# Soft mixture of eight experts: all seven outer products of a Strassen-Winograd scheme split on a second level, as 110 equal tasks

## The chip, the cores and the metric

The kernel runs on one core of a Trainium2 chip. The metric is the device time of one execution in microseconds (us); the median of several executions is compared. Engines are named as in the profile: PE (TensorE matmuls), PEld (its weight loads), DVE (VectorE), ACT (ScalarE), POOL (GpSimd) and SP (SyncE). POOL and SP also issue the DMAs; a DMA that casts or that adds to its destination is issued on POOL.

## The reference

```python
x: [16, 512, 512] f32, router_logits: [16, 512, 8] f32, expert_weights: [8, 512, 2048] f32
probs = softmax(router_logits)                     # over the 8 experts
for e in range(8):
    output += probs[:, :, e:e+1] * np.matmul(x, expert_weights[e])    # [16, 512, 2048] f32
```

Seen as one product: out [8192 rows, 2048] = A [8192, 4096] times B [4096, 2048], where A holds the eight copies of x, each row scaled by that row's probability of the expert, and B holds the experts' weights one above the other. Matmuls run in f16 with sums in f32.

## The kernel before

**The outer scheme.** Rows are taken in half blocks of 256 (`HQ`), an even and an odd one to each of 16 row blocks `q` (or `i`); the experts are cut into two halves (p1 for the first four experts, p2 for the last four, pq for their sum), the columns into two halves of 1024. That is a 2x2 by 2x2 block product, computed with seven block products P1 to P7 instead of eight (Strassen-Winograd). The left factors are products of x and probabilities (`z` tiles in f16, made on DVE from `xT` and `pT`) and differences of these; the right factors are the weights B11, B12, B21, B22 and the sums T1 = B12-B11, T2 = B22-T1, T3 = B22-B12, T4 = T2-B21 (signs as the code has them). P1 uses B11, P2 B21, P5 T1, P6 T2, P3 B22, P4 T4, P7 T3.

**The inner level.** A block product of 256 rows by 1024 columns over two pairs of experts can be split again in the same way, into seven products of 128 rows by 512 columns over 8 steps of 128, 56 matmuls of 128x512 instead of the plain 64. This needs sums of the left factors (`s1`, `s2`, `s4`) and of the weights (`inner_sums`, `inner_weights`: four sums of 128x4096).

**What is split before.** Of the seven products, P1 (from q=2 on), P5, P2 and P4 run one after another through `sub_product`, each with the inner level, over pairs of half blocks; results go to DRAM (`kept` 1, 5 and 2, and P4's into `out`). The first 128 matmuls (q=0,1 of P1) are plain. While a product runs, the generator `prep` of the next one (`weights_of_t1`, `weights_of_21`, `weights_of_t4`, `weights_of_main`) loads expert weights through POOL (with a cast to f16), makes the T sums in tiles of 128x4096 and stores those that are wanted later. `pinned` is False here: the scheduler orders DVE and ACT.

Then `for q in range(NI)` (16 row blocks, `pinned` True, order written by hand) runs P6 and P7 plain, 64 matmuls each, and P3 with the inner level (plain in q=0): 184 matmuls a row block. Kept results are read back by SP (`load_kept`), added in PSUM seeds (ACT) or on DVE (`tt`), and `put` (line 594) sends the outputs, on POOL's queue; the block (1,0) is added to P4's result by an accumulating DMA, 64 in all.

**Names and lines in the profile.** Line 122 is `tt`, every two-operand operation of DVE; 142 is `mm`, the matmuls; 133 `sp` and 136 `pool` are DMAs of the two queues; 404, 627, 649, 669, 718 and 729 are copies by ACT. `w` are weight tiles (15 buffers of 128x4096 f16), `z` left factors (10 buffers of 128x2048 f16), `h` f32 results and seeds, `ps` banks of PSUM, `xT` and `pT` the transposed x and the probabilities.

Of the kernel before, what the change touches and what calls it, by code (L numbers as in the profile page):

```python
# [11 lines left out]
def kernel(  # L33
# [6 lines left out]
):  # L40
    nc = tc.nc
    P = 128
# [10 lines left out]
    NB = 512  # L53
# [12 lines left out]
    zpool = ctx.enter_context(tc.tile_pool(name="zpool", bufs=10))  # L66
# [11 lines left out]
    def share(**sizes):  # L78

        order = sorted(used, key=used.get)  # L80
        for use, n in sizes.items():
            places[use], order = [order[:n], 0], order[n:]
# [26 lines left out]
    pinned = [True]  # L109

# [3 lines left out]
    def dve(i):  # L114
        note(i)
        if pinned[0]:
            tc.keep_in_program_order(i)

    act = dve
# [15 lines left out]
    def pool(o, i):  # L135
        note(nc.gpsimd.dma_start(out=o, in_=i))  # L136
# [9 lines left out]
    stored = {}  # L146
# [3 lines left out]

    def cast_w(q, kn, e, t, parts=1):
        k, n = kn
        for c in range(0, C, C // parts):
            pool(t[:, ds(e * C + c, C // parts), :],
                 expert_weights[(q // 10 - 1) * HE + 2 * k + e, ds(c * P, C * P // parts),
                                ds((q % 10 - 1) * NH + n * NB, NB)].rearrange("(c p) n -> p c n", p=P))

    def load(what, kn, gate=True):
        t = new_w()
        if gate:  # L160
            dve(nc.vector.memset(t.rearrange("p (e c) n -> p e c n", e=2)[:, :, 0, 0:2], 0.0))  # L161
        if (what, kn) in stored:
            pool(t, stored[what, kn])
        else:
            for e in range(2):
                cast_w(what, kn, e, t)
        return t

    def store(what, kn, t):
        stored[what, kn] = d = dram.tile([P, K8, NB], f16, name=f"wd{what}_{kn[0]}{kn[1]}")  # L170
        sp(d, t)

    def inner_sums(b, t3=None):

        t3 = t3 or b[0, 1]
        w = {1: b[0, 0], 2: b[1, 0], 3: b[1, 1], 7: t3}

        def step(p, x, y):
            if p not in w:
                w[p] = new_w()  # L180
            tt(w[p], x, y, SUB)
        return w, [lambda: step(5, b[0, 1], b[0, 0]), lambda: step(6, b[1, 1], w[5]),
                   lambda: step(4, w[6], b[1, 0]), lambda: step(7, b[1, 1], b[0, 1])]

    def inner_weights(b):
        w, sums = inner_sums(b)
        sums[0]()
        yield
        sums[1]()
        sums[2]()  # L190
        yield
        sums[3]()
        return w

# [16 lines left out]
    P2, P1, PQ = 0, HE, 2 * HE  # L211

# [37 lines left out]
    def diag(p):  # L250

        d = h_tile([P, 4, P], f16)
        tt(d, ident.unsqueeze(1).to_broadcast([P, 4, P]), p.to_broadcast([P, 4, P]), MUL)
        return d
# [39 lines left out]

    R = 4
# [21 lines left out]

    x_dram = {}
# [14 lines left out]
    def store_x():  # L333
        while x_new:
            h, xT = x_new.pop()
            x_dram[h] = dram.tile([P, C, HQ], f16, name=f"x_{h}")
            sp(x_dram[h], xT)

# [5 lines left out]
    def mul(xT, pT, e0, ne, t0, nt):  # L344
        z = zpool.tile([P, ne, C, nt], f16, name="z", tag="z")
        tt(z, xT[:, :, ds(t0, nt)].unsqueeze(1).to_broadcast([P, ne, C, nt]),
           pT[:, ds(e0, ne), ds(t0, nt)].unsqueeze(2).to_broadcast([P, ne, C, nt]), MUL)
        return z.rearrange("p e c t -> p (e c) t")


    kept = {r: [dram.tile([2, HQ, NB], f32, name=f"kept{r}_{i}") for i in range(NI)] for r in (1, 2, 5)}

    def half(use="any"):
        return h_tile([P, NB], f32, use)

    def out_rows(i, odd, u, cols, n):
        return out_f[ds((2 * i + odd) * HQ + u * P, P), ds(cols * NH + n * NB, NB)]

    def to_kept(r, i, u, n, t):
        if r == 4:  # L360
            sp(out_rows(i, 1, u, 0, n), t)
        else:
            sp(kept[r][i][n, ds(u * P, P), :], t)

    def from_kept(r, i, u, n, use):
        t = half(use)
        sp(t, kept[r][i][n, ds(u * P, P), :])
        return t

    def sub_product(r, odd, first, w, prep, start=0, xp=None, rest=()):  # L370

        for d in range(start, NI // 2):
            hs = [4 * d + odd, 4 * d + 2 + odd]
            xp = xp or [(load_x(h), load_p(h, first)) for h in hs]
            a11, a12 = (mul(*xp[0], e0, 2, 0, HQ) for e0 in (0, 2))
            a21, a22 = (mul(*xp[1], e0, 2, 0, HQ) for e0 in (0, 2))
            xp = None

            def new(a, b, op):
                z = zpool.tile([P, K8, HQ], f16, name="z", tag="z")  # L380
                tt(z, a, b, op)
                return z
            s1 = new(a21, a22, ADD)
            s2 = new(s1, a11, SUB)
            s4 = new(a12, s2, SUB)
            tt(a21, a11, a21, SUB)
            for make in rest:
                make()
            rest = ()
            z = {1: a11, 2: a12, 3: s4, 4: a22, 5: s1, 6: s2, 7: a21}  # L390

            for u in range(HQ // P):
                banks = {}

                def prod(p, b, start=True):
                    if start:
                        banks[b] = bank()
                    for k in range(K8):
                        mm(banks[b], z[p][:, k, ds(u * P, P)], w[p][:, k, :], start and k == 0, k == K8 - 1)
                    return banks[b]  # L400

                def keep(ps):
                    t = half("r")
                    nc.scalar.copy(t, ps)  # L404
                    return t

                def put(t, n, a, b, op):
                    o = half("o")
                    tt(o, a, b, op)
                    to_kept(r, 2 * d + t, u, n, o)  # L410

                r1 = keep(prod(1, "x"))
                put(0, 0, prod(2, "b"), r1, ADD)
                r5 = keep(prod(5, "q"))
                r2 = keep(prod(6, "x", False))
                put(0, 1, prod(3, "q", False), r2, ADD)
                prod(7, "x", False)
                r3 = keep(banks["x"])
                put(1, 1, banks["x"], r5, ADD)
                put(1, 0, r3, prod(4, "d"), SUB)  # L420
            with behind():
                store_x()
                next(prep, None)
        for _ in prep:
            pass

    ready = {}


    def finish(g):  # L430
        try:
            while True:
                next(g)
        except StopIteration as e:
            return e.value
# [5 lines left out]
    early_z0(1, ds_[1])  # L441
    for n in range(2):
        ps = [bank() for _ in range(4)]
        for e in range(HE):
# [8 lines left out]
            if n == 1:  # L453
                for j in ((4, 5), (6, 7), (), ())[e]:
                    early_xp1(j, ds_[j - 4])
                if e == 1:
                    sums[0]()
        for j in range(4):
            o = half()
            act(nc.scalar.copy(o, ps[j]))  # L460
            sp(kept[1][j // 2][n].rearrange("(p j) m -> j p m", j=2)[j % 2], o)
        if n == 0:
# [3 lines left out]
            w, sums = inner_sums(b11, new_w())  # L466

    def weights_of_t1():
        b = {}
        for i, kn in enumerate(BLOCKS):  # L470
            b[kn] = load(12, kn)
            yield
            tt(b[kn], b[kn], b11[kn], SUB)
            store("t1", kn, b[kn])
        yield
        ready[5] = yield from inner_weights(b)
    pinned[0] = False
    x_new.extend((4 + 2 * t, xp1[t][0]) for t in range(2))
    share(xs=3, r=4, o=8)
    sub_product(1, 0, P1, w, weights_of_t1(), 1,  # L480
                xp1, (sums[1], sums[3], sums[2]))


    def weights_of_21():
        b = {}
        yield
        for kn in BLOCKS:
            b[kn] = load(21, kn)
            yield
            store(21, kn, b[kn])  # L490
        yield
        ready[2] = yield from inner_weights(b)
    sub_product(5, 1, PQ, ready[5], weights_of_21())


    def weights_of_t4():
        b = {}
        for i, kn in enumerate(BLOCKS):
            t, t2 = load(22, kn), load("t1", kn)
            if i < 3:  # L500
                b[kn] = load(21, kn)
            yield
            tt(t2, t, t2, SUB)
            store(22, kn, t)
            store("t2", kn, t2)
            if i == 3:
                b[kn] = load(21, kn)
                yield
            tt(b[kn], b[kn], t2, SUB)
# [263 lines left out]
```

## Time and profile before

| | |
|---|---|
| times of three executions | 1432.79, 1433.21, 1433.62 us, median 1433.21 |
| span of the profiled execution | 1431.8 us |
| median time less that span | 1.4 us |
| granted clock of TensorE | 1.000 |
| matmuls 128x512 / 128x256 (z and w) | 6544 / 16 |
| DMA | 318.92 MB, mean 223 GB/s |

The profile is of one execution; its span runs from the first to the last instruction, and the execution as timed is taken as 1.4 us longer. Shares of busy time are averages over the stages, so the stages are read by windows. In a group's line the first number after the bar is the total of busy time in us, the second the mean of one instruction in ns, and behind the next bar stand the idle time before such instructions and what ended it.

### The profile page before, as it was taken

The page shows a single profiled execution, that of the slowest core. Times are in us where ns is not written, and L with a number is a line of the kernel's source. Part 1 is how long each engine was busy: PE and PEld are TensorE (multiplying, and loading weights), DVE is VectorE, ACT ScalarE, POOL GpSimd, SP SyncE. Part 2 cuts the span into 40 slices and gives each one's busy share as a digit, 9 for nine tenths or more (in the row PEclk, how much of TensorE's full clock was granted, in tenths as well). Part 3 has the DMA queues.
Part 4 walks back from the last instruction along what each step waited for, and adds up shares of the span by engine and source line. Part 5 has one row for each costly group of instructions (what it writes and reads, how often), then busy time and mean ns, then how long its engine had stood idle before and what let it go on. Part 6 is the DMA issues. An engine that isn't in the chain of part 4 may idle for free.

```text
span 1431.8 us, 18014 instructions
## 1 busy us (share of the span) xinstructions
PE 1424.9 (100%) x6654; PEld 648.0 (45%) x6654; DVE 1031.8 (72%) x1177; ACT 271.0 (19%) x472; POOL 220.0 (15%) x344
## 2 busy tenths in 40 slices
PE   9999999999999999999999999999999999999998
PEld 4444444444444444444444444444444444444444
DVE  6967585657686867766767687777777877877773
ACT  3211111111111111111111211111111111111111
POOL 3111100110001000001000222222222222222220
PEclk9999999999999999999999999999999999999999
DMA  9899967899649994367875977787877777778774
GB/s 196 182 252 267 273 160 192 183 256 262 204 148 305 350 333 155 132 186 220 219 250 179 311 218 232 235 239 230 229 231 223 206 216 215 225 234 241 215 199 103
DMA packets 192041, 318.92 MB, mean 223 GB/s; under 512 B 51664, under 2 KB 80592, under 8 KB 187344
## 3 DMA queue, kind: packets, MB, share of 16 engines
q1 hardware_dynamic: 135328, 202.92, 45.2%
q0 software_dynamic: 56624, 114.84, 34.1%
q8 instruction: 52, 0.85, 0.2%
q14 instruction: 37, 0.30, 0.1%
HBM read 180.13 MB, written 159.58 MB: 237 GB/s over the span
## 4 chain that ended last, share of the span: by engine, by line
PE 98%; DMA 1%; POOL 0%; DVE 0%; issue 0%; POOLq 0%
PE ps L142 98%; DMA w<-in_expert_weights_dram 1%; POOL w L136 0%; DVE z L122 0%; DVE h L122 0%; POOL ident L235 0%; POOLq L235 0%; POOLq L757 0%
## 5 line engine op out<-in xcount | busy, mean ns | idle before, releaser
L142 PE MATMUL ps<-w,z 128*128 128x512 f16 x6560 | 1415.2, 379 | 1.2 <-DMA w<-in_expert_weights_dram 0.9
L142 PEld LDWEIGHTS <-z 128*128 128x128 f16 x6560 | 641.6, 98 | 773.6 <-DVE z L122 1.1
L122 DVE TENSOR_TENSOR h<-ps,h 128x512 f32<-128x512 f32 x389 | 268.0, 689 | 328.5 <-PE ps L142 94.4
L122 DVE TENSOR_TENSOR z<-xT,pT 128x2048 f16<-128x2048 f16 x252 | 304.2, 1218 | 32.6 <-PE ps L142 31.2
L122 DVE TENSOR_TENSOR z<-z 128x2048 f16<-128x2048 f16 x280 | 303.6, 1108 | 7.3
L404 ACT COPY h<-ps 128x512 f32<-128x512 f32 x248 | 145.3, 586 | 602.0 <-PE ps L142 596.0
L594 POOL DMA_DIRECT2D out_dram<-h x244 | 154.1, 666 | 516.2 <-DVE h L122 305.5
L122 DVE TENSOR_TENSOR w<-w 128x4096 f16<-128x4096 f16 x36 | 82.3, 2286 | 0.4 <-DMA w<-wd 0.3
L669 ACT COPY h<-ps 128x512 f32<-128x512 f32 x64 | 37.5, 586 | 178.0 <-PE ps L142 176.3
L136 POOL DMA_DIRECT2D h<-in_x_dram x30 | 21.3, 711 | 264.0 <-DMA xT<-h 212.0
L122 DVE TENSOR_TENSOR h<-h,ps 128x512 f32<-128x512 f32 (+1 forms) x78 | 52.7, 676 | 11.1 <-PE ps L142 10.5
L136 POOL DMA_DIRECT2D w<-in_expert_weights_dram x41 | 30.7, 763 | 187.0 <-DVE w L161 130.8
L649 ACT ACTIVATE ps<-h 128x512 f32<-128x512 f32 x35 | 21.0, 601 | 147.0 <-DVE h L122 146.5
L122 DVE TENSOR_TENSOR h<-h 128x512 f32<-128x512 f32 (+1 forms) x67 | 45.9, 684 | 3.6 <-DMA h<-kept 3.5
L627 ACT COPY ps<-h 128x512 f32<-128x512 f32 x64 | 35.5, 593 | 52.5 <-DMA h<-kept 52.5
L136 POOL DMA_DIRECT2D w<-wd x12 | 6.5, 545 | 206.0 <-DVE w L161 132.7
L729 ACT COPY h<-ps 128x512 f32<-128x512 f32 x15 | 8.8, 586 | 120.7 <-PE ps L142 120.7
L718 ACT COPY h<-ps 128x512 f32<-128x512 f32 x15 | 8.8, 586 | 17.1 <-PE ps L142 17.1
L136 POOL DMA_DIRECT2D w<-wdt x8 | 4.4, 555 | 21.9 <-DVE w L161 21.9
L260 DVE CAST z<-ps 128x512 f16<-128x512 f32 x8 | 5.2, 686 | 3.5 <-PE ps L142 3.4
L260 DVE CAST xT<-ps 128x512 f16<-128x512 f32 x4 | 2.6, 686 | 5.9 <-PE ps L142 5.9
L142 PEld LDWEIGHTS <-w 128*128 128x128 f16 x80 | 5.0, 98 | 2.6 <-DMA w<-in_x_dram 0.9
(37 smaller groups left out, 44.6 us busy)
## 6 DMA issues: line engine op xcount, KB each, us to landing
out_dram<-h POOLq DMA_DIRECT2D x244, 256.0 KB, 4.8
kept<-h SPq DMA_DIRECT2D x192, 256.0 KB, 4.3
h<-kept SPq DMA_DIRECT2D x192, 256.0 KB, 4.5
pT<-p_dram SPq DMA_DIRECT2D x124, 256.0 KB, 4.9
w<-in_expert_weights_dram POOLq DMA_DIRECT2D x39, 512.0 KB, 13.1
out_dram<-h SPq DMA_DIRECT2D x75, 256.0 KB, 3.5
xT<-x SPq DMA_DIRECT2D x62, 256.0 KB, 3.1
w<-wd POOLq DMA_DIRECT2D x12, 1024.0 KB, 11.1
```

Of the source, the lines that this page charges most:

```text
L122: dve(nc.vector.tensor_tensor(out=o, in0=a, in1=b, op=op))
L136: note(nc.gpsimd.dma_start(out=o, in_=i))
L142: nc.tensor.matmul(ps, z, w, start=start, stop=stop, skip_group_check=True)
L260: dve(nc.vector.tensor_copy(o, ps))
L404: nc.scalar.copy(t, ps)
L594: queue.dma_start(out=out_rows(self.q, odd, tn[0], cols, tn[1]), in_=o, **how)
L627: act(nc.scalar.copy(x, rows.m1[tn]))
L649: act(nc.scalar.mul(banks[b], v, scale))
L669: act(nc.scalar.copy(c21, x))
L718: act(nc.scalar.copy(r1, x))
L729: act(nc.scalar.copy(r3, x))
```

## The change

- The hand-ordered main loop and `sub_product` go. A `Task` is one outer product of one row block, split by the inner level: always seven products of 8 matmuls, in the order 1, 5, 6, 2, 7, 3, 4. There are 110 tasks; only P1's q=0,1 stay plain.
- Stages: P1 alone for q=2 to 7 and P1 with P2 alternating for q=8 to 15 ("I"); P2 for q=0 to 7; one P5, one P6; then P6 with P5 in pairs ("II"); sixteen P3 ("III"); one P4, one P7; then P7 with P4 in pairs ("IV").
- In a pair the second task takes the results of the first as `seeds` straight from the tiles in SBUF. Elsewhere seeds are loaded by SP, from `kept1` or, in stage III, from `out`. In stage III the left factor also needs s1 = x(odd)·pq, which P5 and P6 stored to DRAM (`s1_dram`, 32 stores and 32 loads of 512 KB).
- Results are summed in `out` by accumulating DMAs on POOL (136 instead of 64).
- Left factors: `zpool` has 6 buffers instead of 10; the four inner sums of a task are made one by one in 128x1024 (`s`, a pool of 7). Seeded tasks add six times from PSUM on DVE.
- Weight sums are made in halves of 128x2048. T1 to T4 and B22 are made in 16 pieces of 128x1024 (`piece`) while P1 and P2 run, kept in DRAM and fetched again when their product comes.
- Every DVE and ACT instruction is held in program order. That order is written out at build time by a planner (`side`, `do`), which has costs for PE and DVE and puts preparation (`prep`), weight sums (`wsum`) and pieces (`rest`) between the evacuations; what a product still lacks is emitted just before it.

The core of the diff:

```diff
-    zpool = ctx.enter_context(tc.tile_pool(name="zpool", bufs=10))
+    zpool = ctx.enter_context(tc.tile_pool(name="zpool", bufs=6))
+    spool = ctx.enter_context(tc.tile_pool(name="spool", bufs=7))
...
+    MULT, SUM2, SUM1, SUMW, EVAC, PROD = 1.22, 1.11, 0.69, 1.17, 0.69, 1.726
+    now = {"pe": 0.0, "dve": 0.0}
+    prep, wsum, rest = deque(), deque(), deque()
+
+    def side(until):
+        while True:
+            for line in (prep, wsum, rest):
+                if line and line[0][0] <= now["pe"] and now["dve"] + line[0][1] <= until:
+                    break
+            else:
+                return
+            do(line)
...
+        def half(p, x, y, i, o=None):
+            if i == 0:
+                made[p] = o if o is not None else new_w()
+            rows = ds(i * C, C)
+            tt(made[p][:, rows], x()[:, rows], y()[:, rows], SUB)
...
+            elif r == 6:
+                s1, t = {}, {}
+                s1_here[self.group, self.q] = s1
+                for k in range(2):
+                    add(prep, MULT, lambda k=k: product(s1, k, names[:2]))
+                    add(prep, MULT, lambda k=k: product(t, k, names[2:]))
+                    add(prep, SUM2, lambda k=k: minus(k, s1, t, t))
+                if self.group == "II":
+                    add(prep, 0.0, lambda: self.keep_s1(s1))
...
+            def prod(p, name):
+                start = name not in b
+                if start:
+                    b[name] = bank()
+                while p not in self.z:
+                    do(prep)
+                while p not in self.w:
+                    do(wsum)
+                now["pe"] = max(now["pe"], now["dve"] if p == 1 else 0.0)
+                for k in range(K8):
+                    mm(b[name], self.z[p][:, k], self.w[p][:, k, :], start and k == 0, k == K8 - 1)
+                now["pe"] += PROD
+                side(now["pe"] + 0.3)
...
+            prod(1, "x")
+            b["b"] = bank()
+            if sd:
+                evac(b["b"], b["x"], sd[q11], ADD)
+            else:
+                act(nc.scalar.copy(b["b"], b["x"]))
+            prod(5, "q")
+            if sd:
+                evac(new(q22), b["q"], sd[q22], ADD)
+            else:
+                copied(q22, b["q"])
+            prod(6, "x")
+            if sd:
+                evac(new(q12), b["x"], sd[q12], ADD)
+            else:
+                copied(q12, b["x"])
+            prod(2, "b")
+            copied(q11, b["b"])
+            self.put(q11, o[q11])
+            prod(7, "x")
+            b["d"] = bank()
+            if sd:
+                evac(b["d"], b["x"], sd[q21], ADD)
+            else:
+                act(nc.scalar.copy(b["d"], b["x"]))
+            evac(o[q22], b["x"], o[q22], ADD)
+            self.put(q22, o[q22])
+            prod(3, "q")
+            evac(o[q12], b["q"], o[q12], ADD)
+            self.put(q12, o[q12])
+            prod(4, "d")
+            copied(q21, b["d"])
+            self.put(q21, o[q21])
...
+    LEAD1, LEAD2, LAG2, LEAD4 = 8, 1, 2, 1
...
+    def piece(kn, j, at):
...
+        def fetch():
+            t["a"], t["b"] = fresh("pab"), fresh("pab")
+            pool(t["a"], w_rows(12, kn, e, c, 2))
+            pool(t["b"], w_rows(22, kn, e, c, 2))
+        def one():
+            d = fresh("pd")
+            tt(d, t["b"], t["a"], SUB)
+            to("T3", d)
+            to("B22", t["b"])
+        def two():
+            tt(t["a"], t["a"], b11[kn][:, rows], SUB)
+            to("T1", t["a"])
+        def three():
+            tt(t["b"], t["b"], t["a"], SUB)
+            to("T2", t["b"])
+            if kn == (0, 1):
+                pool(t["a"], w_rows(21, kn, e, c, 2))
+        def four():
+            tt(t["a"], t["a"] if kn == (0, 1) else b21[kn][:, rows], t["b"], SUB)
+            to("T4", t["a"])
...
+        if t.group == "P2" and t.q == LEAD1 - 3:
+            while rest:
+                do(rest)
+            b5 = {kn: fetch_w("T1", kn) for kn in BLOCKS}
+            bind(5, inner_w(b5))
...
+        if i == first5:
+            b6 = {kn: fetch_w("T2", kn) for kn in BLOCKS}
+            bind(6, inner_w(b6))
+        if i == last6 + 1:
+            b3 = {kn: fetch_w("B22", kn) for kn in BLOCKS}
+            bind(3, inner_w(b3))
...
+        if i == first3:
+            b4 = {kn: fetch_w("T4", kn) for kn in BLOCKS}
+            bind(4, inner_w(b4))
+        if i == first4:
+            share(o=15)
+            b7 = {kn: fetch_w("T3", kn) for kn in BLOCKS}
+            bind(7, inner_w(b7))
+        if i + 1 < len(tasks):
+            if i + 2 < len(tasks):
+                tasks[i + 2].load()
...
+            tasks[i + 1].load_late()
+            tasks[i + 1].prepare()
+        t.run()
```

## The prediction

> **What bounds the kernel now.** I read the page's busy shares first, then the chain of waits in order of time, then the groups by line and shape, then windows.
>
> ```profile
> PE 1424.9 (100%) x6654; PEld 648.0 (45%) x6654; DVE 1031.8 (72%) x1177; ACT 271.0 (19%) x472; POOL 220.0 (15%) x344
> ```
> ```profile
> 18.28 27.82 PE ps L142 x140
> 46.10 0.78 issue
> 46.88 1.23 DVE z L122
> 48.11 0.05 issue
> 48.16 1379.81 PE ps L142 x6400
> 1427.97 0.02 issue
> 1427.99 0.42 DVE h L122
> ```
>
> The reader is to see that TensorE (PE) is the clock of the kernel: apart from two microseconds at 46 one unbroken run of matmuls sets the end. That run holds 6400 instructions, 16 of them of half width, so 6392 full ones: 1379.81/6392 = 0.2159 us each. A change is worth the matmuls it removes times 0.2159, less the time in which PE is made to wait. The work beside PE has prices in the groups:
>
> ```profile
> L122 DVE TENSOR_TENSOR z<-xT,pT 128x2048 f16<-128x2048 f16 x252 | 304.2, 1218 | 32.6 <-PE ps L142 31.2 <-issue 1.4
> L122 DVE TENSOR_TENSOR h<-ps,h 128x512 f32<-128x512 f32 x389 | 268.0, 689 | 328.5 <-PE ps L142 94.4 <-ACT h L669 73.1 <-issue 67.7
> L122 DVE TENSOR_TENSOR z<-z 128x2048 f16<-128x2048 f16 x220 | 263.6, 1222 | 6.3
> L122 DVE TENSOR_TENSOR w<-w 128x4096 f16<-128x4096 f16 x36 | 82.3, 2286 | 0.4 <-DMA w<-wd 0.3
> L122 DVE TENSOR_TENSOR z<-z 128x1024 f16<-128x1024 f16 x60 | 40.0, 688 | 1.0
> ```
>
> (Columns: shapes and count, busy us and mean ns, idle time before.) Three windows (both queues full; SP's transfers alone; one row block q of the main loop) give the load on DMA. Their columns are busy us of PE, PEld, DVE, ACT and POOL, then PE's clock, DMA's busy share and GB/s:
>
> ```profile
> 480.00:500.00 20.00, 20.00 (x94) 9.07 (x93) 14.78 (x16) 4.10 (x7) 2.59 (x4) 1.00 1.08 345
> 570.00:620.00 50.00, 50.00 (x233) 22.69 (x232) 39.29 (x39) 9.45 (x17) 0.00 (x0) 1.00 0.37 127
> 1200.00:1239.70 39.70, 39.70 (x186) 17.99 (x184) 30.71 (x36) 6.84 (x12) 10.03 (x16) 1.00 0.77 225
> ```
>
> The clock is 1.00 everywhere. DMA moves 345 GB/s when both queues are full, and PE does not wait even then.
>
> **What is removed: matmuls.** The built kernel keeps the 128 plain ones of q=0,1 and runs 110 tasks of 7x8 = 6160, 6288 against 6552. The plain part of P1 ends at 40.75 (33.84, where its second half starts, plus 32x0.2159). Without a wait PE would end at 40.75 + 6160x0.2159 = 1370.5, against 1427.97: 57.5 us won.
>
> **What is added: work on DVE per task.** A task lasts 56x0.2159 = 12.09 us on PE. Its DVE bill by the rows (small sums "s" of 128x1024 at 0.667 = 40.0/60, evacuations at 0.689): T1 is 2 products, 4 sums, 2 evacuations: 2.4+2.7+1.4 = 6.5. T2 has six evacuations: 9.2. T6 makes s1 and a11, subtracts, sums and evacuates six times: 4.9+2.4+2.7+4.1 = 14.1, T5 beside it reuses s1: 6.8, pair 20.9 of 24.2. T7 11.4 with T4 9.2: 20.6 of 24.2. In these stages (T1 with T2, P2, T6 with T5, T7 with T4) I cost DVE at nothing; matmuls cover it, and with that cover gone it would cost the excess. T3 is 2 products, 2 subtractions of the s1 read back, 4 sums, 6 evacuations: 11.6 of 12.09. There product 5 waits for sum s5, which is ready 3.7 us into a round whose product 1 gives 3.45: 0.26 us a task, 4.2 us in 16.
>
> **Where DVE is over-booked.** Every change of product needs four weight sums, in eight halves of 2.286/2 = 1.14, 9.1 us. DVE now runs in the written order, so a forced sum holds evacuations and the next task's products behind it, and PE waits for those. From the built order:
> - Start of T1(q=2): one pair of halves before the first task, 2.3 us.
> - P5 to P6: between the starts of T5(0) and T6(1) DVE must do T6(0)'s and T6(1)'s preparation (10.0 each), the last four halves of W5 (4.6), all of W6 (9.1), and evacuations of T5(0) and T6(0) (1.4+4.1): 39.2 us beside 24.2 of PE. 15.0 us.
> - Into stage III (T3): its sums mostly fit in the slack of the pairs; two halves do not. 1.8 us.
> - P4 and P7: between T4(0) and T7(1) all of W4 and W7 (18.3), preparation of T7(0) and T7(1) (20.0), 4 evacuations (2.8): 41.0 beside 24.2. 16.8 us.
> The lower bound of each is zero (DVE ahead by as much), the upper is the figure plus a cast's landing. I take the figures, because six z buffers instead of ten leave no room to run ahead. Together with III: 2.3+15.0+4.2+1.8+16.8 = 40.1.
>
> **Transfers.** The weights T1 to T4 and B22 are now made in 16 pieces beside T1 and T2, and DVE waits in order for casts of 256 KB; behind it are the products of the next task, and PE behind those. By the built order some five and a half places matter, with a cover of about 6 us each, so the price is 5.5x(landing - 6.0). The nearest rows are the x casts of the same 256 KB: 6.7 us median in 50 to 175, 5.6 in 175 to 300, 9.8 in 300 to 360. At 6.7: 3.9 us. Bounds: 0 and 39, the latter at 13.1, the landing of the 512 KB casts. The expert loads pass POOL's queue behind output DMAs there, which only issue (0.54 each).
>
> Stage III reads s1 (1 MB), seeds and x, p back and writes four tiles: 14 units of 256 KB a task, 224, and 16 to 32 units of weights for T4 and T7 beside them. At 0.76 us a unit (67.1 MB at 345 GB/s) 256 units take 194.5 us beside some 198 of PE; at the 0.83 that the SP transfers of the main loop cost, 240 units take 199 and all 256 take 212. Bounds 0 and 14; I take 4, near the full-queue row, since nothing of the 0.83 window was queued full. [...]
>
> Accumulating output DMAs on POOL double to 136. In the main-loop window POOL's queue is busy 39.3% of 39.7 us for 16 outputs, four accumulating; with plain ones at 0.76 (36.6% of 50 us for 24 units in the window 570 to 620) the accumulating cost (15.6-9.1)/4 = 1.6 us. A T7/T4 pair has eight: 12.8 + 5x0.8 = 16.8 of 24.2, hidden, and 8x0.87 us of issue on POOL is hidden too. They bind only from 2.5 us each.
>
> **The end.** Before, 3.8 us lie between the last matmul and the span's end. After: copy by ScalarE 0.59, issue 0.87, landing 4.6 (accumulating outputs in the last 28 us), some 0.25 between: 6.3.
>
> **Sum.** 1370.5 + 40.1 + 3.9 + 4 + 6.3 = 1424.8 of span. Executions last 1.4 us longer than the span shown (median 1433.2 against 1431.8): 1426.2, so 1426, 0.5% faster: most of the matmuls' gain is given back.
>
> The waits are short, 1 to 2.6 us each, as forced sums come in pairs. The 0.78 us gap at 46.10 leaves the granted clock at 1.00 in the window 46 to 50, so I cost no clock loss. [...]
>
> **Rivals.**
> (A) No stalls: DVE runs ahead and PE stays unbroken. 1370.5+6.3+1.4 = 1378, with the start's 2.3 and III's 4.2 1385. For it: DVE is busy only 72%, and the windows show 22 of 25 at worst; against it: the two sums above overrun by 15 and 17 us in the written order. A half-way version (a lead of half a task at both changeovers) gives about 1412. Chance 0.12.
> (B) Slower: DVE held in order behind late weight casts while the pieces are made (120 to 400 us). Without its 3.9 us the sum is 1422; no change is reached at 11 us of loss, landing 8.0; slower by over 0.2% from 14 us, landing 8.6; at 13.1 it gives 1461. For it: 9.8 us in the window 300 to 360, and this stage stores five kept weights as well; against it: the pieces' casts are half as large, and landings were 5.6 to 6.7 in the windows that hold most of them. Chance 0.22.
> (C) DMA binds in stage III or in the accumulating stage: 0.83 a unit over all 256 gives 10 us more, 1436; 0.96 gives 246 us against 198, near 1470. Chance 0.08.
> (D) The change doesn't do what it says: the built instruction counts show 264 fewer matmuls, so I give it nothing.
>
> **How the numbers follow.** The forecast case has 0.58, with an own range of 1412 to 1438: stalls between 30 and 45, transfers between 3 and 13. Less than 0.2% (2.9 us), about what a measurement of this kernel can tell from no change, lies between 1430.3 and 1436.1. The forecast case gives 0.38 faster, 0.12 same, 0.08 slower; A 0.12 faster; B and C 0.03 same, 0.27 slower. Faster 0.50, same 0.15, slower 0.35. The range takes half of A's half-way version and B up to a landing near 12: 1404 to 1456.
>
> **What would show it.** Right: matmul pace 0.216 unchanged; PE waits for DVE (z, s and w) of about 15 us near 400 to 450 and 17 us near 900 to 1000; DVE busy about 85 to 88%; stage III near 198 us. Wrong: PE unbroken at the changes of product (A); the 120 to 400 window longer by tens of us with DVE waiting for weight DMAs (B); DMA share over 1 throughout III with PE waiting for seeds or s1 (C); a pace above 0.216, or a granted clock below 1.00 after a wait.

## The result and the profile after

The changed kernel takes 1490.5 us (median, 1486.9 to 1494.6) against 1433.0 in the same comparison: 1.040 times as long, 95% interval 1.038 to 1.042. The forecast was 1426, with a range of 1404 to 1456. The profiled execution shown here took 1494.6, the slowest of the four, and its span is 1492.9; single executions of this kernel differ by 8 us, those of the kernel before by 0.8.

In the changed kernel's views line 115 is `tt`, 126 the plain DMAs that SP issues (`SPq`), 129 the DMAs of POOL, 135 `mm`, 292 the DMA transposes of x on SP, and 514, 521 and 540 copies by ACT; in the runs the lines can move by a few. `wdT` are the stored T sums, `wdB` the stored B22, `kept` and `out_dram` results; `h` stands for casts, pieces and results alike.

The page's busy times, and the windows by stage (columns as before: busy us and instructions of PE, PEld, DVE, ACT and POOL, then clock, DMA share, GB/s):

```profile
PE 1398.4 (94%) x6382; PEld 623.2 (42%) x6382; DVE 1150.9 (77%) x1492; ACT 216.1 (14%) x375; POOL 294.8 (20%) x440
```
```profile
50.00:425.00 375.00, 333.90 (x1486) 147.46 (x1485) 247.91 (x349) 61.31 (x106) 44.23 (x63) 0.96 0.99 257
450.00:530.00 80.00, 62.40 (x252) 25.58 (x250) 60.67 (x71) 7.58 (x13) 13.97 (x22) 0.89 0.94 257
530.00:835.00 305.00, 305.00 (x1415) 138.25 (x1414) 248.89 (x329) 29.29 (x50) 61.45 (x111) 1.00 0.78 240
835.00:915.00 80.00, 76.23 (x350) 33.89 (x349) 70.39 (x90) 7.61 (x13) 20.23 (x38) 1.00 1.00 372
915.00:1035.00 120.00, 115.93 (x532) 51.06 (x530) 106.39 (x133) 11.13 (x19) 19.56 (x37) 1.00 0.89 297
1075.00:1125.00 50.00, 34.60 (x136) 12.96 (x135) 41.98 (x44) 8.02 (x14) 12.05 (x15) 0.93 0.59 111
1125.00:1475.00 350.00, 350.00 (x1623) 158.70 (x1622) 280.80 (x348) 68.10 (x117) 99.37 (x116) 1.00 0.75 136
```

PE is no longer unbroken. How to read a loss here: the weight loads (second count) are the matmuls of the stretch; what it is longer than their number times 0.2159 is lost. In 50 to 425 (P1, P1 with P2, P2): 375 - 1485x0.2159 = 54.4 us. In 450 to 530 (P5, P6): 26.0. In 1075 to 1125 (P4, P7): 20.9. In stage III, 915 to 1035: 5.6. The steady pairs, 530 to 835 and 1125 to 1475, lose nothing, and 350/1622 = 0.2158 is the pace as before. With 4.7 at the start of III (835 to 915) and 2.8 elsewhere the losses come to 114.4, and 1370.5 + 114.4 = 1484.9 is where the last matmul ends.

Two kinds of loss stand in these lines: PE waits, and the clock below 1.00. Taken apart by the distances between the starts of matmuls, 91.5 us are waits and 23.0 are matmuls at half the clock: 11.4 of the 54.4, 6.9 of the 26.0, 4.2 of the 20.9.

The waits of the stretch 50 to 425, by what the instruction waited for (us in total, times, longest), SP's queue first, then POOL, DVE, ACT and PE. Only the lines used below are shown:

```profile
SPq L126 <- DMA h<-in_expert_weights_dram: 73.2, 15, 8.8
SPq L126 <- DMA x<-xT: 15.0, 4, 6.0
SPq L292 <- DMA x<-xT: 10.1, 1, 10.1
```
```profile
POOL h L129 <- DMA xT<-h: 108.4, 10, 16.0
POOL h L129 <- DMA wdT<-h: 87.0, 17, 12.3
```
```profile
DVE h L115 <- ACT ps L540: 39.4, 7, 12.1
DVE h L115 <- DMA wdT<-h: 33.2, 9, 12.1
DVE h L115 <- DMA h<-in_expert_weights_dram: 26.4, 4, 11.2
```
```profile
ACT h L514 <- DMA kept<-h: 32.2, 8, 11.2
```
```profile
PE ps L135 <- DVE ps L115: 31.0, 9, 10.1
PE ps L135 <- ACT h L514: 7.8, 2, 4.9
```

The first line is the one the prediction lacks: SP, which issues every store of this stretch, stands 73 us waiting for expert casts to land, nearly always before it can store B22. DVE's largest line is mostly a consequence: 31 of its 39.4 us lie before 115, where ACT itself waits up to 8.2 us for result stores. By what DVE or ACT was waiting for just ahead of them, PE's eight longest waits are 17.9 us behind T stores, 10.8 behind casts and 7.7 behind result stores. The longest single wait, in the timeline (start, duration, engine, instruction, idle time before and its releaser):

```profile
160.66 0.71 POOL L129 DMA_DIRECT2D h<-in_expert_weights_dram  x1 [4.21 <-DMA wdT<-h]
...
163.07 0.33 SPq L126 DMA_DIRECT2D wdB<-h  x1
163.50 3.31 SPq L292 DMA_TRANSPOSE xT<-h  x2
...
165.65 1.89 PE L135 MATMUL ps<-w,s 128*128 128x512 f16 x8
...
167.53 0.85 SPq L126 DMA_DIRECT2D wdT<-h  x2
...
172.15 0.69 DVE L115 TENSOR_TENSOR h<-w,h 128x1024 f16<-128x1024 f16 x1 [12.11 <-DMA wdT<-h]
...
176.90 0.69 DVE L115 TENSOR_TENSOR ps<-ps,h 128x512 f32<-128x512 f32 x1
...
177.65 3.57 PE L135 MATMUL ps<-w,s 128*128 128x512 f16 x8 [10.11 <-DVE ps L115]
```

SP issues a B22 store only at 163.1, then transposes of x, then at 167.5 two T stores. DVE stands 12.1 us, from 160.0, at `four`, because it overwrites a tile that is still to be stored as T1. Of these, 3.0 pass before the B22 store goes, 4.5 with the transposes and a load of p, and 4.6 until the T1 store has landed. Behind `four` are the evacuations, and PE gets its bank at 177.6, 10.1 us late. The eight matmuls after the wait then take 3.57 us instead of 1.89: the clock is halved (0.5 in the trace from 171.9 to 182.2).

### The profile page after: what moved, and what is told of

Same layout as the page of the kernel before. It is cut to its first block, busy times and chain, and to the rows that moved or that the text cites. A ratio compares the mean times of both kernels' runs of the same rounds, so it can differ in the third digit from the quotient of the medians.

```text
span 1492.9 us, 17771 instructions
## 1 busy us (share of the span) xinstructions
PE 1398.4 (94%) x6382; PEld 623.2 (42%) x6382; DVE 1150.9 (77%) x1492; ACT 216.1 (14%) x375; POOL 294.8 (20%) x440
## 5 line engine op out<-in xcount | busy, mean ns | idle before, releaser
L135 PE MATMUL ps<-w,z 128*128 128x512 f16 x3648 | 839.6, 382 | 38.0 <-DVE w L115 16.1
L135 PE MATMUL ps<-w,s 128*128 128x512 f16 x2640 | 619.4, 383 | 46.0 <-DVE ps L115 27.5
L135 PEld LDWEIGHTS <-z 128*128 128x128 f16 x3648 | 358.1, 98 | 482.3 <-issue 33.3
L135 PEld LDWEIGHTS <-s 128*128 128x128 f16 x2640 | 258.8, 99 | 372.4 <-issue 47.8
L129 POOL DMA_DIRECT2D out_dram<-h x328 | 221.2, 681 | 726.8 <-ACT h L514 540.3
L115 DVE TENSOR_TENSOR z<-z 128x1024 f16<-128x1024 f16 (+1 forms) x206 | 192.5, 934 | 5.4 <-DMA z<-s 3.2
L115 DVE TENSOR_TENSOR ps<-ps,h 128x512 f32<-128x512 f32 x156 | 108.9, 698 | 74.8 <-PE ps L135 68.0
L115 DVE TENSOR_TENSOR s<-s,z 128x1024 f16<-128x1024 f16 x110 | 75.8, 690 | 2.8
L115 DVE TENSOR_TENSOR s<-z 128x1024 f16<-128x1024 f16 x110 | 75.5, 686 | 1.7
L115 DVE TENSOR_TENSOR s<-z,s 128x1024 f16<-128x1024 f16 x110 | 75.2, 684 | 0.0
L115 DVE TENSOR_TENSOR h<-h 128x1024 f16<-128x1024 f16 (+2 forms) x39 | 26.7, 690 | 29.4 <-DMA h<-in_expert_weights_dram 26.4
L115 DVE TENSOR_TENSOR h<-w,h 128x1024 f16<-128x1024 f16 x12 | 8.3, 690 | 33.2 <-DMA wdT<-h 33.2
```

What stands on the lines that cost most here:

```text
L115: dve(nc.vector.tensor_tensor(out=o, in0=a, in1=b, op=op))
L129: note(nc.gpsimd.dma_start(out=o, in_=i, **how))
L135: nc.tensor.matmul(ps, z, w, start=start, stop=stop, skip_group_check=True)
```

## The experiments

All times are medians, with the ratio to the kernel before and its 95% interval.

**Without B22 stores (e1).** The pieces do not store B22; stage III loads it from the input (`raw_w` fills a tile by two casting loads of 512 KB).

```diff
             to("T3", d)
-            to("B22", t["b"])
...
-            b3 = {kn: fetch_w("B22", kn) for kn in BLOCKS}
+            b3 = {kn: raw_w(22, kn) for kn in BLOCKS}
```

> B22 is not stored by the pieces (16 stores of 256 KB on SP's queue are gone); stage III takes it by a casting load from the input instead. Theory Q (order in the queues): in the changed kernel SP waits 73 us in 15 places for a cast of expert weights to land, nearly all before a B22 store, and result stores, T stores and transposes stand behind it; 54.6 us over the matmul pace are lost between 50 and 425. Without these stores at least half of that goes: 1455 to 1468 us. Theory L (casts land late and DVE itself waits for them, the slower rival of the prediction): the stores are no part of it, under 10 us go: 1481 to 1492 us.

Measured: 1476.2, 1.029 (1.027 to 1.031). Its first window and SP's waits in it:

```profile
50.00:425.00 375.00, 353.02 (x1608) 157.76 (x1606) 269.54 (x377) 63.71 (x110) 45.27 (x65) 0.99 1.01 261
```
```profile
SPq L126 <- DVE h L115: 72.2, 80, 8.2
SPq L126 <- ACT h L520: 40.7, 29, 5.6
SPq L126 <- DMA x<-xT: 16.4, 4, 6.1
```

SP's wait for casts is gone and the loss is 375 - 1606x0.2159 = 28.3 instead of 54.4: 26 us belong to those sixteen stores. The runs below agree: three that keep the stores and the pieces (e3, e4, e8) lose 53 to 56 us there, and e9, which does without, 28.3. Two rivals are settled by the traces. That the stores only loaded the DMA engines: the share is as high without them (1.01 against 0.99) and the landings are no shorter (casts 7.2 us in the median against 6.9, T stores 5.4 against 5.2). That a B22 store held its tile too long: in the changed kernel neither DVE nor POOL ever waits for one to land. What falls is the waiting behind SP's other stores:

```profile
DVE h L115 <- DMA wdT<-h: 12.6, 4, 5.4
ACT h L520 <- DMA kept<-h: 14.9, 5, 7.7
PE ps L135 <- DVE ps L115: 14.5, 9, 3.0
```

Before, these were 33.2, 32.2 and 31.0. So it is the stores' place in SP's order. The total fell short of what was expected by theory Q: the casting loads made PE wait 6.7 us in one place before stage III, with more at the half clock after it, and the changed kernel's profiled execution is 4 us slower than its median.

**Without pieces (e2).** `lines += piece(...)` is dropped and raw weights are loaded for T1 to T4 and B22.

> The 16 pieces are left out altogether (no casts, sums or stores for T1 to T4 and B22); P5, P6, P3, P4 and P7 take the experts' raw weights by casting loads in place of the T sums, so the result is another one. Both theories Q and L: the loss between 50 and 425 falls from 54.6 us to under 15: 1440 to 1455 us. If it does not fall, the loss is not of the pieces but of the x casts, transposes and result stores alone (theory X): 1480 us or more.

Measured: 1476.4, 1.030 (1.029 to 1.032). The first window loses 375 - 1674x0.2159 = 13.6 us, as both theories had it; the total missed the expectation because the casting loads, which read f32 where the fetches read f16, arrive late at the other stages (28 us lost in 835 to 1035 instead of 10, and 10 in 530 to 835 instead of none; in the changed kernel, from 50 to 425, a casting load of 512 KB landed in 12.3 us in the median and a fetch of 1024 KB in 9.7). So pieces cost 41 of the 54 us, and 13.6 remain without any, 11 of them before 115, where x casts, transposes and result stores share the queues with the B21 loads; which of them costs it is not shown.

**Without the forced sums (e3).** `bind(6, inner_w(b6))`, and the same for 4 and 7, take raw blocks in place of sums.

> The inner weight sums of W6, W4 and W7 are left out (raw blocks are used in their place, so the result is another one): 24 half sums of 1.2 us less on DVE. Theory D (DVE over-booked at the changes of product): of 26.0 us lost at P5 and P6 (6.9 of it at the half clock) and 21.1 at P4 and P7 (4.2 of it), 40 or more go: 1443 to 1452 us. Rival W (the weights of T2, T4 and T3 land late there and the sums only stood in the way): less than half goes: 1468 to 1485 us.

Measured: 1457.9, 1.017 (1.015 to 1.019).

```profile
450.00:530.00 80.00, 72.71 (x322) 31.68 (x320) 62.98 (x79) 8.76 (x15) 16.03 (x26) 0.96 1.07 314
1075.00:1125.00 50.00, 50.00 (x234) 22.65 (x232) 40.01 (x50) 11.68 (x21) 17.92 (x21) 1.00 0.88 171
```

At P4 and P7 the whole 20.9 us are gone (50 - 232x0.2159 = -0.1); at P5 and P6 the loss is 10.9 instead of 26.0. Theory D holds, with 36 us in these windows (33 of the time) instead of the 40 expected. Of the rest at P5, PE's longest wait (4.0 us) stands behind W5's sums, which this run keeps, and a wait of DVE that the changed kernel has too:

```profile
DVE z L115 <- DMA pT<-p_dram: 3.4, 1, 3.4
```

In the changed kernel this load of p was issued on SP at 459.4, behind two transposes of together 4.7 us.

**Leads of three (e4).** Three single tasks of each product give the sums room.

```diff
-    LEAD1, LEAD2, LAG2, LEAD4 = 8, 1, 2, 1
+    LEAD1, LEAD2, LAG2, LEAD4 = 8, 3, 2, 3
```

> Three P5 and three P6 tasks instead of one each before the pairs, and three P4 and three P7. Theory D: the sums of W6 and W7 find room in unseeded P5 and P4 tasks (6.5 of 12.1 us on DVE), the loss of 47 us at the two changes falls to 20 to 30: 1462 to 1475 us. Rival (single P6 tasks of 14.1 us on DVE beside 12.1 of matmuls, and more accumulating outputs, give it back): 1480 to 1500 us.

Measured: 1471.1, 1.026 (1.025 to 1.028): as theory D had it. From 450 to 835 and from 1075 to 1125 some 26 us are lost instead of 47.

**B22 cast straight to DRAM (e5)**, with the leads of three: eight DMAs from the input to the stored copy, written in stage II.

```diff
+        if t.group == "II" and t.r == 6 and t.q in (5, 6, 7, 8):
+            kn = BLOCKS[t.q - 5]
+            for e in range(2):
+                pool(kept_w["B22", kn][:, ds(e * C, C)], w_rows(22, kn, e, 0, C))
```

> Three single tasks each of P5, P6, P4 and P7 as in the run before with these leads, no B22 stores on SP, and B22 is cast from the input to its DRAM copy by eight DMAs on POOL during stage II, where no buffer waits for them. Theory Q (SP's order): the 26 us that the run without B22 stores won between 50 and 425, and the 19 us of the leads, add up, and the 7 to 9 us that the casting loads cost at stage III stay won: 1441 to 1450 us. Rival L: the two overlap (the lost time only moves): 1458 to 1470 us.

Measured: 1465.9, 1.022 (1.020 to 1.024), rival L's range, but not for its reason. These DMAs wait for nothing, and the scheduler put them at the head of POOL's queue:

```profile
28.45 0.73 POOL L129 DMA_DIRECT2D wdB<-in_expert_weights_dram  x1 [0.68 <-DMA w<-in_x_dram]
...
62.60 0.70 POOL L129 DMA_DIRECT2D h<-in_x_dram  x1 [18.19 <-DMA xT<-h]
...
93.34 3.15 PE L135 MATMUL ps<-w,z 128*128 128x512 f16 x7 [18.71 <-ACT h L514]
```

The x cast at 62.6, which in the next run is issued at 46.7, makes PE wait 18.7 us through transposes and result stores on SP. **Held in their place (e9)**, `with behind():` around the call:

> As the run with B22 cast directly, but the eight DMAs are held in their place of POOL's order, in stage II; in that run they had gone to the head of POOL's queue, and the x casts came late (an 18.9 us wait at 74). Theory Q: the two gains add up, 26 us for the B22 stores and 19 for the leads: 1441 to 1450 us. Rival: stage I loses as much again for another reason: 1455 to 1466 us.

Measured: 1449.4, 1.012 (1.010 to 1.013). The gains of the two edits add up: 41 of the 45 us expected at the best.

**Result stores on ACT's queue (e6)**, made on the kernel whose B22 DMAs ran too early (`nc.scalar.dma_start` for P1's and P2's results).

> As the run with B22 cast directly, and P1's and P2's results are stored by DMAs that ACT issues, not SP. Theory Q: what is left in 50 to 425 (29 us in the run without B22 stores) is ACT waiting for result buffers whose stores stand on SP behind transposes and T stores; 12 to 22 us of it go, so that much less than the run with B22 cast directly. Rival: ACT, now waiting for DVE at a store, copies late and PE waits for that instead: no gain or up to 10 us slower than that run.

Measured: 1476.7, 1.031 (1.028 to 1.034), 11 us slower than that kernel, as the rival had it to within a microsecond, though ACT waited for something else:

```profile
70.90 1.99 SPq L126 DMA_DIRECT2D kept<-h  x4
...
75.30 0.35 ACTq L132 DMA_DIRECT2D kept<-h  x1
75.74 0.57 ACT L543 COPY ps<-ps 128x512 f32<-128x512 f32 x1 [27.12 <-DMA kept<-h]
76.35 0.69 DVE L115 TENSOR_TENSOR h<-ps,h 128x512 f32<-128x512 f32 x1 [26.44 <-ACT ps L543]
...
79.43 3.58 PE L138 MATMUL ps<-w,z 128*128 128x512 f16 x8 [26.28 <-DVE w L115]
```

ACT stands 27 us at its own first store, which waits for the landing of earlier result stores; these go out on SP only at 70.9, behind transposes of the late x casts. DVE and PE stand behind ACT. Between 115 and 425 it loses 18 us, that kernel 22. A gain of 4 there, and not the 12 to 22 expected, does not make result stores on SP a cost of size; on a kernel without the late x casts it was not tried.

**Zero matmuls (e8).** Five matmuls by a tile of zeros ahead of a product for each forced half sum in P5, P6, P4 and P7.

```diff
+                for k in range(5 * forced):
+                    mm(b[name], zeros, self.w[1][:, 0, :], start and k == 0, False)
```

> The changed kernel with matmuls by a zero tile, five (1.08 us) for each half weight sum that is forced in P5, P6, P4 and P7, put ahead of the product that waits for it; the result is the same. Theory G (the half clock after idle time is a cost of its own): PE is not idle in these waits, the 11.1 us over pace at the half clock in 450 to 530 and 1075 to 1125 fall to 0 to 3, the waits themselves stay: 1478 to 1484 us. Rival: the half clock hid inside waits for DVE, and filling them costs or saves nothing: 1487 to 1495 us.

Measured: 1497.8, 1.044 (1.042 to 1.046).

```profile
450.00:530.00 80.00, 70.11 (x311) 30.56 (x310) 60.42 (x69) 7.58 (x13) 13.45 (x21) 0.98 0.90 257
1075.00:1125.00 50.00, 43.38 (x196) 18.80 (x195) 36.09 (x38) 7.55 (x13) 11.29 (x14) 1.00 0.46 88
```

The clock rises from 0.89 to 0.98 and from 0.93 to 1.00, and matmuls at half clock cost 3.8 us there instead of 11.1: it was the waits that had lowered it. The time did not follow and lies above both ranges: the 140 zero matmuls cost 30 us of PE and filled only 19 us of waits.

**Pieces and the s1 store**, on e9: the last sum of a piece earlier (e10), with it P5's sum for product 7 in a tile of its own (e11), and with the first the pieces wider apart (e12).

```diff
-        return [..., (at + 30, SUM1, four)]
+        return [..., (at + (30 if kn == (0, 1) else 20), SUM1, four)]      e10, e11, e12
...
-        SUB, lambda: part(0, 1)))
+        SUB, None if own else lambda: part(0, 1)))                         e11
...
-        lines += piece(kn, j, 95.0 + 15.0 * i)
+        lines += piece(kn, j, 80.0 + 18.0 * i)                             e12
```

> As e9, and the last sum of a piece (T4) comes right behind the third in the planner's time instead of 10 us later, except in the four pieces that fetch B21 again. Theory P (pieces live longer than their four buffers allow: two in flight, one started every 15 us, each holding its buffers some 30 us and then its store and the next cast, so that POOL waits for buffers with the x casts behind it): of the 15 to 18 us lost between 115 and 425, 6 to 12 go against e9. Rival: DVE then meets the T1 store of the same buffer earlier and waits for it: no gain, or up to 5 us slower.

> As e10, and the sum for product 7 of the three single P5 tasks gets a tile of its own instead of being written over half of s1, which is on its way to DRAM then; in the changed kernel DVE waits 8.3 us for that store and PE 4 to 6. If that wait is all: 3 to 7 us less than e10, at the start of P5. If the forced weight sums behind it set the time: 0 to 2 us.

> As e10, with the pieces started every 18 us from 80 of the planner's time instead of every 15 from 95. Theory P: the buffers are free when the next cast is due, 3 to 8 us less than e10. Rival: the first pieces now collide with the B21 loads at the start, and it is 0 to 8 us slower.

Measured: 1454.7, 1447.6 and 1465.7 (ratios 1.016, 1.010, 1.023, each to 0.002). Theory P falls: `four` meets the T1 store of its own tile sooner. DVE waits 10.6 us for it up to 324, and its waits for T stores between 100 and 425 rise from 12.1 us in e9 to 33.3. With wider spacing PE waits 8.8 us from 328, behind a late cast, and 8.5 us from 405, behind a T store. The tile of its own is worth 7.0 us. DVE's wait at the start of P5 without it, as it stands in e10:

```profile
DVE z L115 <- DMA s<-z: 8.3, 2, 8.0
```

In e11 there is no such line. Without the tile, product 7's sum is written over s1 while the store of s1 is under way. This wait came with the leads of three (8.6 us in e4, 8.3 in e9); against what the expectation says, the changed kernel itself has none at P5.

**Order of the single tasks (e13)**, and on it two edits for the rest of stage I (e14, e15).

```diff
+    tasks[f + 2], tasks[f + 3] = tasks[f + 3], tasks[f + 2]               e13
...
-    share(xs=2, o=8, pab=4, pd=1)
+    share(xs=3, o=7, pab=4, pd=1)                                         e14
...
-            add(rest, 0.06, lambda kn=kn, e=e: load_b21(kn, e), 50.0 + 6.0 * (2 * i + e))
+            add(rest, 0.06, lambda kn=kn, e=e: load_b21(kn, e), 60.0 + 6.0 * (2 * i + e))      e15
-    add(rest, 0.0, lambda: bind(2, inner_w(b21)), 108.0)
+    add(rest, 0.0, lambda: bind(2, inner_w(b21)), 114.0)                                  e15
```

> As e9 (leads of three, no B22 stores, B22 cast in stage II), with the product 7 sum of P5 in its own tile (7.0 us in e11 against e10) and the single tasks in the order 5, 5, 6, 5, 6, 6 instead of 5, 5, 5, 6, 6, 6: P6 tasks of 14.1 us on DVE follow one another less often, each such step cost 2.9 us in e9. 1449.4 less 7 less 3 to 6: 1436 to 1440 us. If the order makes no difference: 1441 to 1444.

> As e13, with three buffers for casts of x instead of two, and seven for results instead of eight, while the pieces are made. Theory X (what is left between 50 and 425, 29 us in e9, comes from x casts that wait on POOL for one of two buffers, 97 us in nine waits there, with SP held at the transposes): 4 to 12 us less than e13. Rival R (ACT waits for result buffers): seven buffers make it 2 to 10 us slower.

> As e13, with the eight B21 loads (512 KB casts on POOL) and the sums of W2 10 and 6 us later in the planner's time. Theory S (at the start, 40 to 115, 12 us are lost because B21 casts stand ahead of x casts): 2 to 6 us less than e13. Rival: the loads only move into the first pieces and W2 comes late at 128: 0 to 8 us slower.

Measured: 1439.5 (1.004, 1.002 to 1.005), 1438.1 (1.004, 1.002 to 1.005) and 1439.5 (1.005, 1.003 to 1.006). e13 is 9.9 us below e9: 7.0 for the tile of its own, so by subtraction about 3 for the order; single executions of e13 differ by 6, so these 3 are not shown. Neither x buffers nor the B21 loads explain what is left: with three buffers the loss in 40 to 425 is 25.9 us against 27.7; with B21 later, 40 to 115 falls from 12.7 to 7.1 and 115 to 425 rises from 15.0 to 21.5. What holds these 26 us is not settled: each edit moved waits between the queues. No version here is faster than the kernel before; the best is 0.4% slower.

## Why the prediction was wrong

- **Matmuls removed**: right. 6288 instructions, pace 0.2158, no other change of pace in the steady stages.
- **DVE hidden in the steady stages**: right for the pairs, nothing lost in 655 us of II and IV. DVE's share is 77%, not the 85 to 88% named as a sign. Its 1150.9 us would be 81% even of the forecast span, so the bills are somewhat high: 82% and 80% are measured in the two stretches of pairs, 86% and 85% by the bills.
- **Stage III**: 0.61 to 0.62 us a task lost (the distances between matmuls at s5), 0.26 forecast; PE's waits there are for DVE, also in the first 80 us with DMA share 1.00 and 372 GB/s, so the 4 us for DMA were not due. Why DVE is 0.35 us a task later than forecast is open. Forecast for III with its start 10.0, measured 12.2 (835 to 1075).
- **Over-booked DVE**: right in mechanism, place and nearly in size: 15.0 and 16.8 us forecast, waits of 19.1 and 16.9 measured. Of the 4.1 more at P5 and P6, 3.4 can be DVE's wait for a load of p behind transposes on SP, which the prediction does not name; no run took this wait out alone.
- **Transfers, 3.9 us: the step that failed.** With the start's 2.3 us the forecast for 40 to 425 was 6.2; 55.2 were measured. The landing was right: 6.9 us median for the pieces' casts, 6.7 assumed, and the formula gives 5.0 with it. The formula counted only DVE behind casts (26.4 us of DVE's waits, 10.8 us of PE's). It left out that the stores which the pieces issue go through SP in order: a B22 store waits there for its cast, and T stores, transposes and result stores behind it; their buffers then hold DVE, ACT and, through POOL, the next casts. The first experiment shows 26 us of it directly, the second 41 for the pieces as a whole; the 13.6 that stay without pieces have no shown cause. The prediction counted stage I's loads on POOL and no order on SP at all.
- **Clock, 0 us**: 23.0 measured. The prediction's own row misled: the 0.78 us at 46.10 is a piece of the chain through DVE, and the idle time of PE there is 0.33 us (`48.16 12.04 PE L142 MATMUL ps<-w,z 128*128 128x512 f16 x55 [0.33 <-DVE z L122]`), too short to bear on waits of 2 us and more. In the two changes of product the clock was 0.89 and 0.93. The waits after which it was halved lasted 2.2 to 10.3 us, and others of up to 3.1 us did not halve it, so no single length of wait parts the two here.
- **The end**: 7.9 us after the last matmul, 6.3 forecast.
- **Rival B** had the side and the stretch (slower, 120 to 400) but not the mechanism: it needed landings of 8.6 us, and they were 6.9. It had 0.22; its price at the measured landing was 5 us.

The sum redone: 1370.5 + 55.2 + 26.0 + 12.2 + 20.9 + 7.9 = 1492.7 of span. That it closes to 0.2 us shows that no stretch was left out, and not the causes: the losses come from the same trace.

## What to carry to other kernels

For every store that a change adds, ask what it waits for and what stands behind it in its queue: here the B22 stores waited on SP for their casts (73.2 us of waits for casts from 50 to 425) and held the later stores, and the buffers that these would free; without them (e1) 26 us less were lost there. A kernel with an unbroken matmul pace can pay twice for a wait, the wait and the slower clock after it: here 91.5 us and 23.0. An edit that lightens one queue can be undone by a scheduler that moves a free instruction to the queue's head (1465.9 us in e5, 1449.4 in e9); hold it in its place.

## What was not expected of the hardware

- A short wait could lower the clock or leave it: after one of 2.4 us at 364 in the changed kernel, the clock was 0.50 from 366.5 to 369.9, while after one of 3.1 us at 252 it stayed at 1.00.
- In e8, five zero matmuls per forced sum raised the clock (0.89 to 0.98 in 450 to 530), though they compute nothing.
